# Expert layers of a two-block transformer kernel: 40 stored units for 64, one product for four key rows, 28 of 64 gate groups on ScalarE, three parked pairs

## The chip, the cores and the metric

The kernel runs on one core of a Trainium2 chip. Each engine (TensorE, VectorE, ScalarE, GpSimd, and SyncE, which issues the DMAs here) works through a queue of its own in order and waits on semaphores. The metric is the device time of one execution in microseconds (us). In the trace PE is TensorE's matmuls, PEld its weight loads, DVE VectorE, ACT ScalarE, POOL GpSimd and SP SyncE.

## The reference

Two transformer blocks run over 256 tokens of width 1024 in fp32. The change touches the feed-forward part of the first block's two layers, a product-key expert layer with 128 x 128 experts. Cut to that:

```python
def peer_ffn(x, norm_ffn, w_query, sub_keys, expert_down, expert_up):
    xn = rmsnorm(x, norm_ffn)
    def chunk(xi):                      # 128 tokens
        q = (xi @ w_query).reshape(B, 128, 8, 2, 128)
        s = jnp.einsum('bthpd,hpnd->bthpn', q, sub_keys)
        s1, i1 = lax.top_k(s[..., 0, :], 16)
        s2, i2 = lax.top_k(s[..., 1, :], 16)
        cand = s1[..., :, None] + s2[..., None, :]
        top_s, top_c = lax.top_k(cand, 16)       # over the 256 sums
        idx = i1[top_c // 16] * 128 + i2[top_c % 16]
        g = softmax(top_s)
        u = expert_down[idx]
        act = gelu(einsum('btd,bthkd->bthk', xi, u))
        return einsum('bthk,bthkd->btd', g * act, expert_up[idx])
```

`first_block` is mixer, expert layer, mixer, expert layer; `second_block` has gated feed-forward layers and further mixers, and its modulation vectors come from products with `w_mod`.

## The kernel before, in words

The kernel does not gather experts. `peer` computes all 16384 of them for all tokens and weights them with a dense gate matrix that is zero where an expert was not chosen. Experts are cut into 128 **units** of 128; unit `i` holds the experts whose second key index is `i`. A unit of `down` or `up` weights is 128x1024 fp32 (512 KB). `Stream.unit` loads it into one of three `raw` buffers, rounds it to `whi` on ScalarE (L93) and puts the remainder into `wlo` on VectorE (L97). `mm3` (L170 to L172) multiplies by three products, high by high, high by low and low by high, so a unit is 24 matmuls of 256 columns on TensorE, for `down` (tile `dn`) and for `up` (tiles `acc`) alike.

One expert layer runs in four parts.

1. **Routing.** Sixteen query units, scores, and on VectorE a long run of top-16 searches that ends with `it`: for each token, in 128 rows (8 heads by 16 picks), the first index, the second index and the gate.
2. **Stored units.** The first `N_STORE` down units are computed in pairs, beside the routing and behind it. ScalarE's gelu writes each pair into `ca`. They need no routing result.
3. **Gate stage.** 64 groups of four tokens. For a group, `oa` (VectorE, L631) holds one-hot rows of the first index, `ob` one-hot rows of the second index times the gate. `ob` is made by VectorE (L636) or, in the groups marked `by_act`, by two ScalarE operations a token (L633, L634). TensorE multiplies `oa` by `ob` into a PSUM bank `gps` (L639), four matmuls that the trace shows as eight records. Then VectorE multiplies the stored columns of `ca` by the first `N_STORE` columns of `gps` (L641), in place, so the first such product waits for the last stored unit; ScalarE copies the other columns to `gg` (L642). `oa` and `ob` have three buffers each, `gps` four banks.
4. **Loop.** The other down units, in pairs: gelu in place in PSUM, multiplied into `gg` (L667). The up units follow at a lag of 16 and are added up in `acc`.

The accumulators of `acc` take the four banks of tag `ac`. Until the loop starts, these serve the stored pairs, then `N_PARK` **parked** pairs (the first pairs of the loop, computed during the gate stage and held in PSUM until `gg` is complete) and one bank for `mod`. `Mod.step` (L935, L940) is one product of a 512 KB piece of `w_mod` through the same three `raw` buffers, four matmuls shown as eight records. Eight steps make a row, which ends with a copy `mrow` (L944) and two transposes (L946). The first expert layer has 32 such steps behind its parked pairs, the second 40.

The order of each engine's queue is not written out: a planner of the framework sets it when the kernel is built, from priorities and a timeline of its own. A loop in the code therefore appears in the queues interleaved with its neighbours.

Of the kernel before, what the change touches and what calls it, by code (L numbers as in the profile page):

```python
# [14 lines left out]
OP = mybir.AluOpType  # L15
# [4 lines left out]
NDC = 8  # L20
EPS = 1e-6
NEG = -1.0e30
N_STORE = 64
N_LAG = 16
N_PARK = 2
N_MOD = 32
M_0 = 40
M_1 = 72
PAT_1 = "gggv"
PAT_0 = "gv"  # L30
M_BUFS = 3
N_ACT = 3
OH = 3
AB = 3
AHEAD = 0
# [452 lines left out]
def peer(n: Net, layer, mod, mod_upto):  # L488
    nc, d = n.nc, n.d
    pre = f"l{layer}_"  # L490
    NS = N_STORE
    n.stream.pattern = PAT_R
    with ExitStack() as st:
        sp = st.enter_context(n.tc.tile_pool(name="pk", bufs=1, reuse_waits="tile"))
        it = sp.tile([128, 3, T], F32, name="it")
# [4 lines left out]
        def down_pair(i, sink, tag=None):  # L500
            b = n.bank("dn", tag).rearrange("p (u t) -> p u t", u=2)
            for u in range(2):
                w = n.unit(d[pre + "down"][i + u])
                n.proj_t(b[:, u], w, xn, first=u == 0)
            sink(b)

        with ExitStack() as sr:
# [44 lines left out]
            for a0, a1, wb, o in CAND:  # L552
                na = a1 - a0
                nc.vector.tensor_tensor(
                    out=cand[:, :, o:o + na * wb].rearrange("p h (a b) -> p h a b", b=wb),
                    in0=v4[:, :, 0, a0:a1].unsqueeze(3).to_broadcast([128, 16, na, wb]),
                    in1=v4[:, :, 1, 0:wb].unsqueeze(2).to_broadcast([128, 16, na, wb]), op=OP.add)
            for h in range(16):
# [6 lines left out]
                                    op=OP.subtract)  # L565
# [15 lines left out]
            for a0, a1, wb, o in CAND[:-1]:  # L581
                run = r.tile([128, 16, 16], F32, tag="run", name="run", bufs=2)
                for i, s0 in enumerate(starts[a0 + 1:a1 + 1]):
                    if i == 0:
                        nc.vector.tensor_scalar(out=run, in0=pos, scalar1=float(s0), scalar2=None, op0=OP.is_ge)
                    else:
                        nc.vector.scalar_tensor_tensor(out=run, in0=pos, scalar=float(s0), in1=run,
                                                       op0=OP.is_ge, op1=OP.add)
# [5 lines left out]
            for s, rank in ((0, ra), (1, rb)):  # L594
                for k0, k1 in ((0, 4), (4, 8), (8, 16)):
# [3 lines left out]
                                            in1=n.iota[:, 0:k1].unsqueeze(1).unsqueeze(1).to_broadcast([128, 16, nk, k1]),  # L599
                                            op=OP.is_equal)  # L600
                    nc.vector.tensor_tensor(out=o, in0=o,
                                            in1=i4[:, :, s, 0:k1].unsqueeze(2).to_broadcast([128, 16, nk, k1]),
                                            op=OP.mult)
# [9 lines left out]
            for i in range(0, NS, 2):  # L613
                down_pair(i, lambda b: nc.scalar.activation(
                    out=ca[:, i:i + 2], in_=b, func=AF.Gelu_apprx_tanh), "ac")

        with ExitStack() as sg:
            gp = sg.enter_context(n.tc.tile_pool(name="gg", bufs=1, reuse_waits="tile"))
            gg = gp.tile([128, 128 - NS, T], F32, name="gg")
            onehot = n.tc.tile_pool(name="oneh", bufs=OH, reuse_waits="tile")  # L620
            o2 = onehot.__enter__()
            for t0 in range(0, T, 4):
                a = o2.tile([128, 4, 128], F32, tag="oa", name="oa")
                b = o2.tile([128, 4, 128], F32, tag="ob", name="ob")
                g = n.bank("gps").rearrange("p (t e) -> p t e", t=4)


                by_act = t0 // 4 % N_ACT == 1
                for t in range(4):
                    at = lambda s: it[:, s, t0 + t:t0 + t + 1]  # L630
                    nc.vector.tensor_scalar(out=a[:, t], in0=n.iota, scalar1=at(0), scalar2=None, op0=OP.is_equal)  # L631
                    if by_act:
                        nc.scalar.activation(out=b[:, t], in_=n.iota, func=AF.Abs, scale=-1.0, bias=at(1))  # L633
                        nc.scalar.activation(out=b[:, t], in_=b[:, t], func=AF.Relu, scale=-2.0, bias=at(2))  # L634
                    else:
                        nc.vector.tensor_scalar(out=b[:, t], in0=n.iota, scalar1=at(1), scalar2=at(2),  # L636
                                                op0=OP.is_equal, op1=OP.mult)
                for t in range(4):
                    nc.tensor.matmul(g[:, t], a[:, t], b[:, t], start=t == 0, stop=True, skip_group_check=True)  # L639
                ge = g.rearrange("p t e -> p e t")  # L640
                nc.vector.tensor_tensor(out=ca[:, :, t0:t0 + 4], in0=ca[:, :, t0:t0 + 4], in1=ge[:, 0:NS], op=OP.mult)  # L641
                nc.scalar.copy(out=gg[:, :, t0:t0 + 4], in_=ge[:, NS:128])  # L642
            n.stream.pattern = PAT_G
            onehot.__exit__(None, None, None)
            g2 = sg.enter_context(n.tc.tile_pool(name="gg2", bufs=2, reuse_waits="tile"))

            def coef(i):
                return ca[:, i] if i < NS else gg[:, i - NS]

            acc = []  # L650

            def up(i):
                if not acc:
                    acc.extend(n.accs())
                w = n.unit(d[pre + "up"][i])
                c = coef(i)
                ch = g2.tile([128, T], F32R, tag="ch", name="ch")
                cl = g2.tile([128, T], F32R, tag="cl", name="cl")
                n.split(c, ch, cl)
                n.up(acc, w, (ch, cl), i == 0, i == 127)  # L660

            done = 0
            for i in range(NS, 128, 2):
                def sink(b):
                    nc.scalar.activation(out=b, in_=b, func=AF.Gelu_apprx_tanh)
                    c = gg[:, i - NS:i - NS + 2]
                    nc.vector.tensor_tensor(out=c, in0=c, in1=b, op=OP.mult)  # L667
                if i == NS + 2 * N_PARK:
                    while mod.next < mod_upto:
                        mod.step(n.main.raw_p)  # L670
                    mod.bank = None
                down_pair(i, sink, "ac" if i < NS + 2 * N_PARK else None)
                while i >= NS + 2 * N_PARK and done < i + 2 - N_LAG:
                    up(done)
                    done += 1
            while done < 128:
                up(done)
                done += 1
            n.residual(n.x, acc)
# [765 lines left out]
def two_blocks_kernel(ctx: ExitStack, tc: tile.TileContext, d, out, stages=None):  # L1445
# [12 lines left out]
    for s in stages:  # L1458
        with tc.tile_pool(name="xn", bufs=1, reuse_waits="tile") as n.xn_p:
            if s in ("mix0", "mix1"):  # L1460
                with n.psum(ac=4, mm=3, fl=1), tc.tile_pool(name="mod", bufs=M_BUFS, reuse_waits="tile") as p:
                    with n.low():
                        aside(mods[0], p, M_0 if s == "mix0" else M_1)
                    (hgrn_gmlp if s == "mix0" else mla_moba)(n)
            elif s.startswith("peer"):
                with n.psum(ac=4, mm=2, m2=2):
                    peer(n, int(s[4]), mods[1], N_MOD if s[4] == "0" else 72)
            elif s.startswith("mod"):
                with n.psum(ac=4, mm=2, fl=2), tc.tile_pool(name="mod", bufs=3, reuse_waits="tile") as p:
                    aside(mods[int(s[3])], p, 72)  # L1470
            elif s.startswith("ffn"):
                w, l = int(s[3]), int(s[5])
                with n.psum(ac=4, mm=2, m2=2):
                    ffn(n, n.x, mods[l], 0, 0 if w == 1 else 6, d[f"f{w}i{l}"], d[f"f{w}o{l}"],
                        n.v(f"norm_g{l}")[:, (w - 1) * 16:(w - 1) * 16 + 8], s)
            elif s == "mixb0":
                with n.psum(ac=4, mm=2, fl=2):
                    window_gla(n, mods[0])
            elif s == "mixb1":
                with n.psum(ac=4, mm=2, m2=2):  # L1480
                    pool_mix(n, mods[1])
            elif s == "final":
                with n.psum(ac=4, mm=2, m2=2):
                    final_norm(n, out)
# [154 lines left out]
```

## Time and profile before

| | us |
|---|---|
| median of three runs | 3464.38 |
| lowest of three | 3463.34 |
| the profiled execution | 3467.64 |
| its span in the trace | 3465.9 |

The profiled execution is 3.3 us above the median, and its span is 1.7 us below its own time. One of the three times, 13268.22 us, is far off and plays no part here. Times below are us from the start of the span. Matmuls are pipelined, so a record's length is more than the time until the next one starts, and a busy share close to 1 can hide slack; idle time and the distances between starts say more.

### The profile page before, as it was taken

The numbers are of one execution on the slowest core, as the hardware profiler recorded it, in microseconds if no ns is written. First come the engines' busy times: TensorE is split into PE (matmuls) and PEld (weight loads), VectorE is DVE, ScalarE is ACT, GpSimd is POOL, SyncE is SP. The second block draws the span as 40 slices with busy tenths as digits, with TensorE's granted clock in tenths as the row PEclk, the third lists the DMA queues.
The fourth block names the chain that finished last, engine by engine and source line by source line (L and its number), as shares of the span: only waits on it lengthen the run. The fifth ranks groups of instructions, "written<-read, shape, count | busy, mean of one in ns | idle before, by whom it ended". The sixth has DMA issues, their size and how long they took to land.

```text
span 3465.9 us, 65621 instructions
## 1 busy us (share of the span) xinstructions
PE 3313.4 (96%) x26734; PEld 3150.2 (91%) x26734; DVE 2193.9 (63%) x4589; ACT 1649.2 (48%) x2609; POOL 179.0 (5%) x93
## 2 busy tenths in 40 slices
PE   7999998999999999998999999999999989999798
PEld 6789977999999779996899999999999779999698
DVE  6389487555556559759555555666766656666665
ACT  5445455444444344445445444544644444454443
POOL 2200000000000310000000000100000020100200
PEclk9999999999999999999999999999999999999899
DMA  6645544556555545545556555554444235454353
GB/s 227 230 159 182 178 156 161 183 183 207 183 183 170 199 157 166 177 158 182 195 183 231 183 183 183 182 183 143 158 165 147 86 123 187 165 183 156 132 187 105
DMA packets 165759, 597.79 MB, mean 172 GB/s; under 512 B 18512, under 2 KB 20176, under 8 KB 165072
## 3 DMA queue, kind: packets, MB, share of 16 engines
q1 hardware_dynamic: 165456, 593.59, 51.5%
q8 instruction: 210, 3.44, 0.4%
q14 instruction: 93, 0.76, 0.1%
HBM read 592.47 MB, written 1.05 MB: 171 GB/s over the span
## 4 chain that ended last, share of the span: by engine, by line
PE 83%; DVE 11%; DMA 2%; ACT 2%; issue 1%; POOL 0%; SPq 0%; ACTq 0%; DVEq 0%; POOLq 0%
PE acc L170 11%; PE acc L171 10%; PE acc L172 10%; PE dn L172 7%; PE dn L170 7%; PE dn L171 7%; PE ff L170 6%; PE ff L171 6%; PE ff L172 6%; DVE wlo L97 2%; PE mm L170 2%; PE mm L171 2%; PE mm L172 2%; PE mod L940 2%; DMA mraw<-w_mod 2%; PE gps L639 2%
## 5 line engine op out<-in xcount | busy, mean ns | idle before, releaser
L93 ACT CAST whi<-raw 128x1024 fp32r<-128x1024 f32 x973 | 1016.3, 1046 | 1398.9 <-PE acc L171 540.7
L97 DVE TENSOR_TENSOR wlo<-raw,whi 128x1024 fp32r<-128x1024 f32 x908 | 1111.6, 1225 | 841.8 <-ACT whi L93 841.3
L170 PE MATMUL dn<-xnh,whi 128*128 128x256 f32 x2048 | 582.3, 284 | 3.1 <-ACT gg L642 2.5
L172 PE MATMUL dn<-xnh,wlo 128*128 128x256 f32 x2048 | 581.8, 285 | 1.5 <-DVE wlo L97 1.5
L171 PE MATMUL dn<-xnl,whi 128*128 128x256 f32 x2048 | 581.5, 284 | 0.0
L171 PE MATMUL acc<-cl,whi 128*128 128x256 f32 x2048 | 561.6, 283 | 1.0 <-DVE cl L165 1.0
L172 PE MATMUL acc<-ch,wlo 128*128 128x256 f32 x2048 | 559.5, 283 | 0.0
L170 PE MATMUL acc<-ch,whi 128*128 128x256 f32 x2048 | 512.2, 283 | 0.2 <-DVE gg L667 0.2
L170 PE MATMUL ff<-xnh,whi 128*128 128x258 f32 x1760 | 504.6, 287 | 7.5 <-ACT rstd L216 4.0
L171 PE MATMUL ff<-xnl,whi 128*128 128x258 f32 x1760 | 502.8, 286 | 4.2 <-DVE xnl L247 4.2
L172 PE MATMUL ff<-xnh,wlo 128*128 128x258 f32 x1760 | 499.2, 284 | 3.5 <-POOL wlo L97 2.2
L170 PEld LDWEIGHTS dn<-xnh,whi 128*128 128x128 f32 x2048 | 395.0, 193 | 3.7 <-ACT gg L642 2.7
L172 PEld LDWEIGHTS dn<-xnh,wlo 128*128 128x128 f32 x2048 | 394.4, 193 | 2.2 <-DVE wlo L97 2.2
L171 PEld LDWEIGHTS dn<-xnl,whi 128*128 128x128 f32 x2048 | 395.0, 193 | 0.0
L171 PEld LDWEIGHTS acc<-cl,whi 128*128 128x128 f32 x2048 | 393.2, 192 | 1.5 <-DVE cl L165 1.5
L172 PEld LDWEIGHTS acc<-ch,wlo 128*128 128x128 f32 x2048 | 392.1, 192 | 0.0
L170 PEld LDWEIGHTS acc<-ch,whi 128*128 128x128 f32 x2048 | 363.7, 192 | 0.4 <-DVE gg L667 0.4
L170 PEld LDWEIGHTS ff<-xnh,whi 128*128 128x128 f32 x1760 | 334.8, 190 | 12.2 <-ACT rstd L216 5.2
L171 PEld LDWEIGHTS ff<-xnl,whi 128*128 128x128 f32 x1760 | 337.0, 192 | 6.3 <-DVE xnl L247 5.6
L172 PEld LDWEIGHTS ff<-xnh,wlo 128*128 128x128 f32 x1760 | 335.1, 191 | 4.9 <-POOL wlo L97 2.7
L97 POOL TENSOR_TENSOR wlo<-raw,whi 128x1024 fp32r<-128x1024 f32 (+1 forms) x65 | 157.7, 2433 | 2614.0 <-ACT whi L93 1968.6
L171 PE MATMUL acc<-hl,whi 128*128 128x256 f32 x880 | 246.9, 282 | 3.0 <-DVE hl L1017 3.0
(446 smaller groups left out, 5389.5 us busy)
## 6 DMA issues: line engine op xcount, KB each, us to landing
raw<-l_down SPq DMA_DIRECT2D x256, 512.0 KB, 3.4
raw<-l_up SPq DMA_DIRECT2D x256, 512.0 KB, 3.3
mraw<-w_mod SPq DMA_DIRECT2D x144, 512.0 KB, 4.4
raw<-f1i SPq DMA_DIRECT2D x132, 512.0 KB, 3.4
raw<-f2i SPq DMA_DIRECT2D x88, 512.0 KB, 3.9
raw<-f1o SPq DMA_DIRECT2D x66, 512.0 KB, 3.3
raw<-w_t SPq DMA_DIRECT2D x46, 512.0 KB, 3.6
raw<-f2o SPq DMA_DIRECT2D x44, 512.0 KB, 4.1
```

Source lines behind the costliest of these rows:

```text
L93: nc.scalar.copy(hi[:, 0:k], raw[:, 0:k])
L97: eng.tensor_tensor(out=low[:, 0:k], in0=raw[:, 0:k], in1=hi.bitcast(F32)[:, 0:k], op=OP.subtract)
L170: mm(out, w[0], x[0], start=first, stop=False, skip_group_check=True)
L171: mm(out, w[0], x[1], start=False, stop=False, skip_group_check=True)
L172: mm(out, w[1], x[0], start=False, stop=last, skip_group_check=True)
L639: nc.tensor.matmul(g[:, t], a[:, t], b[:, t], start=t == 0, stop=True, skip_group_check=True)
L940: nc.tensor.matmul(ps[32 * j:32 * j + 32], n.cond[:, k], raw[:, j * T:(j + 1) * T], start=k == 0, stop=k == NDC - 1, tile_position=(0, 32 ...
```

## The change

`N_STORE` goes from 64 to 40, so 24 down units of each expert layer move from before the gate stage into the loop; `ca` shrinks to 40 columns and `gg` grows from 64 to 88. `oa` is made by one product of 512 elements for a group where there were four of 128. `N_ACT` becomes 7 and the test for `by_act` changes, so ScalarE makes `ob` in 28 of the 64 groups where it made 21; they lie 3, 2, 2, 3, 2, 2, 2 groups apart. `N_PARK` goes from 2 to 3.

```diff
-N_STORE = 64
+N_STORE = 40
 N_LAG = 16
-N_PARK = 2
+N_PARK = 3
...
-N_ACT = 3
+N_ACT = 7
...
                 g = n.bank("gps").rearrange("p (t e) -> p t e", t=4)
...
-                by_act = t0 // 4 % N_ACT == 1
+                by_act = t0 // 4 * N_ACT % 16 < N_ACT
+                nc.vector.tensor_tensor(out=a, in0=n.iota.unsqueeze(1).to_broadcast([128, 4, 128]),
+                                        in1=it[:, 0, t0:t0 + 4].unsqueeze(2).to_broadcast([128, 4, 128]),
+                                        op=OP.is_equal)
                 for t in range(4):
                     at = lambda s: it[:, s, t0 + t:t0 + t + 1]
-                    nc.vector.tensor_scalar(out=a[:, t], in0=n.iota, scalar1=at(0), scalar2=None, op0=OP.is_equal)
                     if by_act:
```

In the changed kernel the lines behind this place are numbered two higher, and `oa` is made in L629.

VectorE's queue in the middle of the first layer's gate stage, before:

```order
L641 TENSOR_TENSOR ca<-ca,gps 128x64x4
L631 TENSOR_SCALAR oa<-iota,it 128x128 x4
L641 TENSOR_TENSOR ca<-ca,gps 128x64x4
L631 TENSOR_SCALAR oa<-iota,it 128x128
L636 TENSOR_SCALAR ob<-iota,it 128x128
L631 TENSOR_SCALAR oa<-iota,it 128x128
```

and after:

```order
L643 TENSOR_TENSOR ca<-ca,gps 128x40x4
L629 TENSOR_TENSOR oa<-iota,it 128x512
L638 TENSOR_SCALAR ob<-iota,it 128x128 x4
L643 TENSOR_TENSOR ca<-ca,gps 128x40x4
L629 TENSOR_TENSOR oa<-iota,it 128x512
L643 TENSOR_TENSOR ca<-ca,gps 128x40x4
```

A group whose `ob` VectorE makes was nine instructions and is six; a group of ScalarE's was five and is two.

ScalarE's queue at about the same place, before:

```order
L633 ACTIVATE ob<-iota,it 128x128 x4
L634 ACTIVATE ob<-ob,it 128x128 x2
L642 COPY gg<-gps 128x64x4
L634 ACTIVATE ob<-ob,it 128x128 x2
L642 COPY gg<-gps 128x64x4 x2
```

and after:

```order
L635 ACTIVATE ob<-iota,it 128x128 x4
L644 COPY gg<-gps 128x88x4
L636 ACTIVATE ob<-ob,it 128x128 x4
L635 ACTIVATE ob<-iota,it 128x128 x4
L644 COPY gg<-gps 128x88x4
L636 ACTIVATE ob<-ob,it 128x128
L644 COPY gg<-gps 128x88x4
L636 ACTIVATE ob<-ob,it 128x128 x3
L644 COPY gg<-gps 128x88x4 x2
```

Before, three copies stand between the start of one gated group and that of the next; now mostly two.

TensorE's queue at the end of the second layer's gate stage, where `dn` is the first pair of the loop, before:

```order
L639 MATMUL gps<-ob,oa 128x128 x2
L940 MATMUL mod<-mraw,cond 32x256 x4
L639 MATMUL gps<-ob,oa 128x128
L940 MATMUL mod<-mraw,cond 32x256 x4
L946 MATMUL mod<-ident,mrow 128x128 x2
L170 MATMUL dn<-xnh,whi 128x256
```

and after:

```order
L641 MATMUL gps<-ob,oa 128x128 x10
L948 MATMUL mod<-ident,mrow 128x128 x2
L641 MATMUL gps<-ob,oa 128x128 x6
L942 MATMUL mod<-mraw,cond 32x256 x32
L948 MATMUL mod<-ident,mrow 128x128 x2
L170 MATMUL dn<-xnh,whi 128x256
```

The last row of `w_mod`, eight steps in one piece, now stands behind the last gate group, where one step stood. In the first layer the last step stays ahead of the last groups. Further up, the twelve `gps` matmuls of the fifth to seventh gate group stand in a row in all four queues (in the trace they are 24 records in a row); ahead of this place the queue of the first layer has 590 `dn` matmuls fewer than before, that of the second 594, and the loop 528 more each. Between this place and the first step of `w_mod` stand 40 `dn` matmuls before, up to the tenth group, and 102 and 106 after, up to the eighteenth.

## Rows read from the trace of the kernel before

**Rows 1.** The page, part 1: busy time of each engine and its instructions.
```profile
PE 3313.4 (96%) x26734; PEld 3150.2 (91%) x26734; DVE 2193.9 (63%) x4589; ACT 1649.2 (48%) x2609; POOL 179.0 (5%) x93
```
**Rows 2.** Stretches: window, length, busy PE, PEld, DVE, ACT, POOL, clock, DMA share, GB/s.
```profile
360.00:440.00 80.00, 80.00 (x669) 80.00 (x669) 33.67 (x29) 36.32 (x42) 0.00 (x0) 1.00 0.54 182
449.50:572.00 122.50, 106.89 (x813) 78.95 (x812) 109.81 (x457) 67.93 (x216) 0.00 (x0) 0.94 0.47 155
1537.50:1658.00 120.50, 107.22 (x849) 75.43 (x847) 106.60 (x455) 65.31 (x213) 0.00 (x0) 0.96 0.51 167
```
**Rows 3.** The chain that ended last, both expert layers: start, length, piece.
```profile
449.53 2.68 PE gps L639 x24
...
575.21 0.38 PE acc L170
...
581.07 0.48 PE acc L170 x4
583.95 0.48 PE acc L170 x4
...
1537.50 2.68 PE gps L639 x24
...
1670.05 0.12 PE acc L170
```
**Rows 4.** Timeline of VectorE in the first gate stage: start, length, instruction.
```profile
519.64 0.86 DVE L631 TENSOR_SCALAR oa<-iota,it 128x128 f32<-128x128 f32 x4
520.42 0.41 DVE L641 TENSOR_TENSOR ca<-ca,gps 128x256 f32<-128x256 f32 x1
520.75 0.27 DVE L631 TENSOR_SCALAR oa<-iota,it 128x128 f32<-128x128 f32 x1
520.95 0.33 DVE L636 TENSOR_SCALAR ob<-iota,it 128x128 f32<-128x128 f32 x1
521.21 0.27 DVE L631 TENSOR_SCALAR oa<-iota,it 128x128 f32<-128x128 f32 x1
```
**Rows 5.** VectorE's groups by shape, 300 to 345 us: count, busy us, mean ns.
```profile
L598 DVE TENSOR_TENSOR oh<-rb,iota 128x2048 f32<-128x2048 f32 x1 | 2.3, 2294 | 0.0
...
L598 DVE TENSOR_TENSOR oh<-ra,iota 128x512 f32<-128x512 f32 x1 | 0.7, 693 | 0.0
```
**Rows 6.** Timeline of ScalarE in the first gate stage.
```profile
524.12 1.28 ACT L633 ACTIVATE ob<-iota,it 128x128 f32<-128x128 f32 x4 [2.88 <-PE gps L639]
525.30 1.26 ACT L634 ACTIVATE ob<-ob,it 128x128 f32<-128x128 f32 x4
526.47 0.62 ACT L642 COPY gg<-gps 128x256 f32<-128x256 f32 x2
```
**Rows 7.** Waits between 445 and 578 us: total us, times, longest.
```profile
ACT ob L633 <- PE gps L639: 25.7, 12, 3.7
...
DVE ca L641 <- PE gps L639: 12.6, 9, 3.0
...
PE mod L940 <- DMA mraw<-w_mod: 7.4, 8, 1.8
```
**Rows 8.** The w_mod row copies of the first stage, and TensorE's timeline of one row.
```profile
L944 DVE COPY mrow<-mod x4: 409/413/419, 477.0 to 548.6; 128x256 f32<-128x256 f32 x4
...
534.92 1.50 PE L940 MATMUL mod<-mraw,cond 128*32 128x256 f32 x24
...
539.30 0.64 PE L940 MATMUL mod<-mraw,cond 128*32 128x256 f32 x8 [0.99 <-DMA mraw<-w_mod]
...
544.96 0.42 PE L940 MATMUL mod<-mraw,cond 128*32 128x256 f32 x4 [1.28 <-DMA mraw<-w_mod]
```
**Rows 9.** End of the second gate stage: a stretch, and TensorE's timeline.
```profile
1660.00:1665.00 5.00, 3.93 (x16) 3.24 (x17) 3.35 (x7) 2.09 (x2) 0.00 (x0) 0.50 0.77 242
...
1657.27 0.64 PE L940 MATMUL mod<-mraw,cond 128*32 128x256 f32 x8
...
1661.21 0.58 PE L170 MATMUL dn<-xnh,whi 128*128 128x256 f32 x1 [0.60 <-ACT whi L93]
```

## The prediction, as made before the run

> **What bounds the kernel now.** I read the page's busy times first, then the stretches, the chain of waits, the timelines of the gate stage. TensorE is busy for 96% of the span [rows 1], so the change can win only where TensorE does no useful work. The stretches show two such places, the gate stages of the two expert layers. In the 80 us ahead of the first stage TensorE is busy throughout at a granted clock of 1.00, while VectorE works for 33.7 us only: routing is over, and the gates wait for stored units. From 449.5 to 572 us it is turned round: VectorE is busy for 109.8 of 122.5 us, ScalarE for 67.9, TensorE's weight loads for 79.0 [rows 2]. So the work that could cover the gate stage is spent before it.
>
> I measure a stage from the place where twelve `gps` matmuls start in a row (fifth gate group) to the first up matmul of `acc`. Before, that is 449.53 to 575.21, 125.7 us, and 1537.50 to 1670.05, 132.6 us [rows 3]. The kernel does the same matmuls after the change, so its gain is what these two stretches lose, corrected for units moved across their ends.
>
> **Moved units.** Twenty-four matmuls take 2.88 us (583.95 less 581.07) [rows 3], 0.12 us each. The 590 `dn` matmuls that leave the place ahead of the first stage free 70.8 us on the path, in full, since TensorE never idles there [rows 2]; the 528 that the loop gets cost 63.4 us. The loop must stay bound by TensorE for that: a pair there gets one gelu and one product more than a stored pair, while VectorE and ScalarE have half their time free beside a TensorE that is full, as in the 80 us above (33.7 and 36.3 busy). I cost these at nothing; without the cover each would be some 0.7 us a pair (a 512-element operation [rows 5]), 8 us a layer. The difference, 62 matmuls or 7.4 us (66 or 7.9 us in the second layer), is the further parked pair, now inside the stage.
>
> **VectorE's share of a group.** Starts lie 0.78 us apart over four pieces of `oa`, 0.26 over a piece of `ob`, 0.33 over `ca` [rows 4]. A group of VectorE's took 0.78 + 1.04 + 0.33 = 2.15 us, one of ScalarE's 1.11; with 43 and 21 of them, 1.81 on average. The one product of 512 elements is not in the trace, but a comparison of the same form is: 693 ns at 512 elements and 2294 at 2048, so 1.042 ns an element [rows 5]. `ca`'s 0.33 for 256 elements then leaves 0.06 for the instruction, and `oa` takes 0.60, `ca` with 160 elements 0.23. Groups now take 1.87 and 0.83, and 36 and 28 of them 1.42 on average: 0.39 less, 23.6 us for the 60 groups behind the mark. Bounds: with 0.69 for `oa` and nothing saved at `ca`, 12 us; 24 is the other end. I take 23.6, since spacing and not length is what repeats.
>
> Here a rule speaks against the edit. The rows give 0.78 for four pieces and 0.60 for the one. The Trainium skill, "VectorE: DVE Perf Modes", section "The perf-mode tier table (the rule you actually need)", says that an fp32 tensor_scalar in SBUF runs at two elements a cycle and an fp32 tensor_tensor at one; its cycle table in the section "The TRN2 errata — SBUF-src ops pay a fixed extra latency per instruction" gives as an estimate 4 x 0.13 = 0.51 us for the pieces and 0.59 for the one. By the page the edit would cost 0.09 a group, not save 0.18, and the forecast below would be 3462. The trace agrees on the one product (the page has 2293 ns at 2048 elements, the row 2294) but not on the pieces, and the row decides.
>
> **ScalarE's share.** Its `ob` for a group takes 2.35 us (524.12 to 526.47), and two `gg` copies 0.62 [rows 6]. Seven more groups add 16.5 us over 64. `gg` grows from 256 elements to 352: nothing if its time is fixed, 0.12 if all of it goes by the element; I take 0.08. Together 0.34 a group, 20 us a stage, so 67.9 becomes some 91 with the whi and gelu of 2.6 further parked units. VectorE's 109.8 becomes 109.8 - 23.6 + 2.9 (wlo of those units, 1024 elements at the slope above) = 89. TensorE has 60 groups at 0.89 (24 records in 2.68 [rows 3]), 53.6 us, 102 `dn` matmuls, 12.2, and 32 steps of `w_mod` at 0.5 (three in 1.50 [rows 8]), 16: 82. So three engines come out nearly level where one stood out.
>
> **What the stage takes then.** Before, VectorE idled 12.7 of 122.5 us; the waits of that stage are VectorE's for TensorE, 12.6 us, and behind them TensorE's for `w_mod`, 7.4 us [rows 7]. Neither goes away. With three level engines, queues in order and three buffers I expect 14 us beside ScalarE's 91: 105 us to the last `ca`. Ends: 8 and 22, so 99 to 113.
>
> First layer: behind the last group the loop's first pair takes 48 x 0.12 = 5.8 us, and 0.7 passes at `gg`, so 111.5 against 125.7. With the 7.4 that is **21.6 us** gained.
>
> Second layer: the last row of `w_mod` now stands behind the last group, uncovered. Three steps are loaded (1.5 us); five more come as the buffers allow, three steps in 5.66 us (539.30 to 544.96, a wait for DMA ahead of both [rows 8]), so 9.4; from the start of the last step to the first `dn` 3.9 passed before (1657.27 to 1661.21 [rows 9]), of which 0.5 is counted. That is 14.3. Before it the granted clock was 0.50 of full speed, 1.2 of 2.4 GHz, while the first pair ran (1660 to 1665), after a TensorE that waited, and the pair took 8.8 us to 1670.05 [rows 3, 9]; it will again. 105 + 14.3 + 8.8 = 128.1 against 132.6, with the 7.9 **12.4 us** gained.
>
> Sum: 34 us. The profiled execution's 3467.64 becomes 3433.6; it lies 3.3 above the median, so on the median 3464.38 - 34 = **3430 us**.
>
> **The rivals.**
>
> *The w_mod stream sets the stage.* The first stage's row copies lie 71.6 us apart from the first to the fourth, 23.9 a row [rows 8], and VectorE needed 12 x 1.81 = 21.7 of it; now its 11.75 groups a row need 16.6. If the stream through three buffers does not get faster than 23.9, four rows take 96 us, and with 25 us for the 14 groups and parked units ahead of them (14 x 0.89 + 12.2) the stage takes 120, 15 more in each layer: 3460. For it: waits for `w_mod` are already there. Against: at three steps in 5.66 us, eight need 15.1, under 16.6.
>
> *The engines overlap well.* If parked pairs fill the waits and only 4 us stand beside ScalarE's 91, the stage takes 95, and the time is 3410. For it: VectorE lost little before. Against: then one engine was the bound, now three are.
>
> *The hand-off through ScalarE becomes the bound: slower.* ScalarE may start a group's `ob` only when the `gps` of three groups earlier has freed the buffer, and before it waited 25.7 us in 12 waits for just that [rows 7]. Most gated groups now lie two apart. If each is done in series, `gps` 0.89, `ob` 2.35, two `gg` at 0.39, `ca` 0.23, two groups take 4.25 us instead of ScalarE's own 3.1, three groups VectorE's 4.55; sixteen groups take 30.4, 60 take 114, and with the 13 of the other waits the stage takes 127: 22 more in each layer, 3474, slower than before. It decides from 122 us a stage on, that is when two groups take about 4.0. Against: the queue starts `ob` a group or two ahead, and a third buffer is there to hide it.
>
> *The one product takes its whole recorded 0.69 us and `ca` saves nothing*, the lower bound above: VectorE is then busy for 101 us, ten more than ScalarE, and with the 14 the stage takes 115, 3450. The two rows on spacing speak against it.
>
> That the change does not do what it says can be left out: the queues show the units moved.
>
> **How the numbers follow.** Forecast 0.55 (3416 to 3447 from the 99 and 113), w_mod stream 0.14, good overlap 0.17, hand-off 0.12, dear product 0.02. For 8 in 10 I take 3402 to 3464: it holds the forecast, the w_mod case and most of the good overlap, and leaves out the hand-off. Two per cent, about what a measurement of this kernel tells from no change, is 69 us. A gain of that size would need both stages at 88 us, under the busy time of their busiest engines: 0.04. A loss of it would need 35 us more in each stage than before: 0.02. Within: 0.94.
>
> **What the profile after would show.** The twelve `gps` some 71 us earlier, near 379 us; `oa` at 0.60 from start to start; TensorE busier and ScalarE's busy share near 0.87 in the stage; from there to the first up matmul 111 us in the first layer and 128 in the second, with eight steps of `w_mod` alone at its end. The forecast is wrong if the time from mark to last `ca` is not near 105: at 120 with TensorE waiting for `mraw` it is the stream, at 127 with TensorE waiting for ScalarE's `ob` the hand-off. It would also be wrong if the loop, now with 40 pairs behind the parked and first ones instead of 29, did not keep TensorE full.

## The result, and the profile after

The changed kernel takes 3427.94 us in the median of five runs (3419.31 to 3431.81), the kernel before 3464.38; the ratio is 0.9889 with an interval of 0.9874 to 0.9904. That is 36 us, 34 were forecast, and it lies inside two per cent. The profiled execution took 3422.14 us, the one before 3467.64: this pair is 45.5 us apart, more than the medians, so the places below add up to 45.5 and not to 36.

TensorE keeps its 26734 matmul records. The page, part 1, against [rows 1]:

```profile
PE 3278.1 (96%) x26734; PEld 3132.8 (92%) x26734; DVE 2157.5 (63%) x4173; ACT 1685.3 (49%) x2721; POOL 177.6 (5%) x93
```

The stretches from the mark (twelve `gps` matmuls in a row) to the last `ca`, and one behind the second stage; columns as in [rows 2]:

```profile
379.20:479.20 100.00, 95.22 (x850) 76.32 (x849) 88.81 (x263) 85.11 (x264) 0.00 (x0) 1.00 0.54 183
1433.60:1534.90 101.30, 94.61 (x859) 76.42 (x857) 88.13 (x263) 84.36 (x264) 0.00 (x0) 1.00 0.53 179
...
1535.00:1555.00 20.00, 11.60 (x86) 5.86 (x82) 6.35 (x12) 4.11 (x6) 0.00 (x0) 0.66 0.78 255
```

The marks and the end of the second stage in the chain, against [rows 3, 9]:

```profile
379.24 2.68 PE gps L641 x24
...
484.83 0.48 PE acc L170 x4
...
1433.64 2.68 PE gps L641 x24
...
1534.51 0.61 PE mod L942 x8
1535.14 4.11 DMA mraw<-w_mod
1539.30 0.68 PE mod L942 x8
1540.00 4.37 DMA mraw<-w_mod
1544.41 1.12 PE mod L942 x8
1545.55 3.27 DMA raw<-l_down
1548.84 1.05 ACT whi L93
...
1558.16 0.12 PE acc L170
```

From mark to first up matmul these are 105.6 and 124.5 us, where 125.7 and 132.6 stood. The reader should see three busy engines in the first two stretches, where VectorE alone stood out before ([rows 2]). The chain of work that ended last says the same: in the first stage VectorE's `oa`, `ob` and `ca` made up 18.6, 16.3 and 8.9% of it before and 1.0% or less each after, when TensorE's `gps` has 31.9%, the loads of `w_mod` 23.0% and ScalarE's `ob` 12.2%. The reader should also see, in the second layer, the eight `w_mod` steps behind the last group, from 1534.51 on: there the chain passes from load to product to load, and the first pair's load of `l_down` comes last (1545.55).

VectorE and ScalarE inside the stage, against [rows 4, 6]:

```profile
426.79 0.68 DVE L629 TENSOR_TENSOR oa<-iota,it 128x512 f32<-128x512 f32 x1
427.39 1.11 DVE L638 TENSOR_SCALAR ob<-iota,it 128x128 f32<-128x128 f32 x4
428.42 0.31 DVE L643 TENSOR_TENSOR ca<-ca,gps 128x160 f32<-128x160 f32 x1
428.65 0.68 DVE L629 TENSOR_TENSOR oa<-iota,it 128x512 f32<-128x512 f32 x1
```

```profile
425.70 0.45 ACT L644 COPY gg<-gps 128x352 f32<-128x352 f32 x1
426.03 0.42 ACT L636 ACTIVATE ob<-ob,it 128x128 f32<-128x128 f32 x1
426.33 0.45 ACT L644 COPY gg<-gps 128x352 f32<-128x352 f32 x1
426.66 1.01 ACT L636 ACTIVATE ob<-ob,it 128x128 f32<-128x128 f32 x3
```

`oa` starts 0.60 us ahead of the next instruction and `ca` 0.23, as the prediction had them; a `gg` copy holds ScalarE for 0.33. The waits between 370 and 490 us, against [rows 7], and the row copies of the first stage, against [rows 8]:

```profile
ACT ob L635 <- PE gps L641: 11.3, 12, 2.2
DVE ca L643 <- PE gps L641: 11.0, 16, 2.0
```

```profile
L946 DVE COPY mrow<-mod x4: 416/416/417, 418.5 to 474.6; 128x256 f32<-128x256 f32 x4
```

VectorE waits about as long as before (12.6 us then), ScalarE less than half (25.7), and a row of `w_mod` takes 18.7 us where it took 23.9.

Outside the stages the trace gives a layer's length by where the last sum of `x` (L209) at its end starts. After:

```profile
L209 DVE TENSOR_TENSOR x<-acc,x x8: 410/412/425, 181.2 to 184.7; 128x256 f32<-128x256 f32 x8
L209 DVE TENSOR_TENSOR x<-acc,x x8: 406/411/424, 1082.8 to 1085.8; 128x256 f32<-128x256 f32 x8
L209 DVE TENSOR_TENSOR x<-acc,x x8: 410/410/419, 1242.1 to 1244.5; 128x256 f32<-128x256 f32 x8
L209 DVE TENSOR_TENSOR x<-acc,x x8: 407/409/412, 2157.6 to 2164.5; 128x256 f32<-128x256 f32 x8
```

So the first expert layer runs from 184.7 to 1085.8, 901.1 us, the second from 1244.5 to 2164.5, 920.0. In the same rows of the kernel before the last sums start at 185.9, 1117.1, 1275.3 and 2209.6: 931.2 and 934.3. The gain is 30.1 us in the first layer and 14.3 in the second; the rest, 1 us, is no part of either.

### The profile page after: what moved, and what is told of

The parts are those of the page before. It is cut to its first block, busy times and chain, and to the rows that moved or that the text cites. A ratio compares the mean times of both kernels' runs of the same rounds, so it can differ in the third digit from the quotient of the medians.

```text
span 3420.4 us, 65219 instructions
## 1 busy us (share of the span) xinstructions
PE 3278.1 (96%) x26734; PEld 3132.8 (92%) x26734; DVE 2157.5 (63%) x4173; ACT 1685.3 (49%) x2721; POOL 177.6 (5%) x93
## 4 chain that ended last, share of the span: by engine, by line
PE 84%; DVE 8%; DMA 3%; ACT 2%; issue 1%; ACTq 0%; DVEq 0%
PE acc L170 11%; PE acc L171 11%; PE acc L172 10%; PE dn L172 7%; PE dn L170 7%; PE dn L171 7%; PE ff L170 6%; PE ff L171 6%; PE ff L172 6%; DMA mraw<-w_mod 2%; PE gps L641 2%; DVE wlo L97 2%; PE mm L170 2%; PE mm L171 2%; PE mm L172 2%; PE mod L942 2%
## 5 line engine op out<-in xcount | busy, mean ns | idle before, releaser
L172 PE MATMUL acc<-ch,wlo 128*128 128x256 f32 x2048 | 566.4, 283 | 0.0
L170 PE MATMUL acc<-ch,whi 128*128 128x256 f32 x2048 | 533.8, 283 | 0.0
L170 PEld LDWEIGHTS acc<-ch,whi 128*128 128x128 f32 x2048 | 373.1, 192 | 0.0
```

The source lines that it names most:

```text
L170: mm(out, w[0], x[0], start=first, stop=False, skip_group_check=True)
L172: mm(out, w[1], x[0], start=False, stop=last, skip_group_check=True)
```

## The experiments

Theory A, the prediction's: VectorE, the busiest engine of the gate stage, sets its length, so an edit is worth what it takes off VectorE, until ScalarE and TensorE are level with it; moved units change little. Rivals: B, the stored units kept back as cover are the gain; C, the `w_mod` stream sets the stage; D, the kernel before merely lost time to stretches at half the granted clock.

All twelve runs, with both kernels. *Stage* is from the start of the first `ca` product to that of the last, both layers (it begins some 4 us ahead of the mark), *VectorE* its busy time in there, *layer* as above, from one trace each; the ratio is to the kernel before on the same chip.

| kernel | stage | VectorE | layer | median | ratio |
|---|---|---|---|---|---|
| before | 125.7, 123.9 | 113.1, 109.9 | 931.2, 934.3 | 3464.38 | 1 |
| before again | 122.4, 123.9 | 113.0, 109.9 | 927.9, 934.1 | 3467.24 (one run) | - |
| before, 40 stored | 113.5, 111.3 | 107.0, 103.7 | 914.4, 925.0 | 3447.72 | 0.9964 (0.9947 to 0.9981) |
| before, one product | 111.0, 108.1 | 103.6, 100.1 | 917.0, 917.5 | 3437.03 | 0.9935 (0.9917 to 0.9954) |
| before, 28 groups | 112.5, 113.5 | 107.2, 104.2 | 918.1, 924.5 | 3448.05 | 0.9950 (0.9929 to 0.9971) |
| before, 3 parked | 120.5, 117.7 | 115.6, 113.0 | 921.1, 931.7 | 3461.62 | 1.0000 (0.9986 to 1.0013) |
| changed | 103.8, 104.5 | 91.8, 91.3 | 901.1, 920.0 | 3427.94 | 0.9889 (0.9874 to 0.9904) |
| changed, 64 stored | 106.0, 106.0 | 96.6, 96.3 | 908.0, 924.7 | 3436.89 | 0.9926 (0.9910 to 0.9942) |
| changed, four pieces | 110.1, 110.8 | 99.3, 99.5 | 915.5, 931.1 | 3451.23 | 0.9969 (0.9955 to 0.9984) |
| changed, 21 groups | 107.6, 103.6 | 99.1, 96.8 | 905.4, 922.5 | 3434.22 | 0.9925 (0.9908 to 0.9943) |
| changed, 32 groups | 112.4, 113.1 | 91.8, 88.6 | 907.0, 918.4 | 3432.28 | 0.9918 (0.9902 to 0.9934) |
| changed, no `w_mod` in layer 1 | 97.2, 103.2 | 90.8, 90.6 | 891.8, 985.7 | 3485.55 (one run) | - |
| changed, row in the mixer | 104.6, 105.2 | 91.9, 91.9 | 900.3, 921.2 | 3431.64 | 0.9904 (0.9887 to 0.9921) |
| changed, row among stored units | 107.9, 105.5 | 92.0, 90.1 | 906.2, 933.0 | 3439.69 | 0.9938 (0.9924 to 0.9951) |

A layer in a single trace can be off by some 5 us: the last kernel has the changed kernel's TensorE order throughout the first layer, and that layer came out at 906.2 against 901.1, its stage at 107.9 against 103.8. Smaller differences are read from the medians.

The columns show something that A leaves out. VectorE's busy time goes down by what the edits take off it: 6.1, 9.5 and 5.9 us for the first three parts alone and 2.5 more for the parked pair, 19.0 together in the first stage, and 21.3 in the changed kernel (18.7 and 18.6 in the second). But each part alone shortens the stage by more than that, because VectorE's idle time in the stage falls as well: from 12.7 and 14.0 us (9.3 and 14.1 in the second execution) to between 4.7 and 9.3. In the changed kernel it is back at 12.0 and 13.1, so the whole gains what comes off VectorE and no idle time.

**The parts one by one.** The units alone:

```diff
-N_STORE = 64
+N_STORE = 40
```

> The kernel before with 40 stored units alone. An expert layer is measured in the trace from the last residual of its mixer to its own: 931.2 and 934.3 us before, 901.1 and 920.0 after the whole change. Theory A (VectorE sets the gate stage, so a part is worth what it takes off VectorE, and moving units across the stage frees as much at one end as it costs at the other): 0.10 us less for ca in 60 groups, 6 us a layer, so about 925 and 928, median 3452. Theory B (the units that were spent ahead of the stage are the gain, since gates start 70 us earlier): at least 25 us in the first layer, 906 or less, median 3430 or less. Theory C (the w_mod stream sets the stage): 0 to 2 us a layer.

3447.72, ratio 0.9964, 12 us. Its stages from mark to last `ca` are 109.9 and 107.6 us, VectorE busy for 103.95 of the first. By the ratio this is A's number, and B's median of 3430 or less is not reached. The first layer of the trace, 914.4 us, lies between the two (A 925, B 906): its stage fell by 12.2 us where VectorE's busy time fell by 6.1.

The one product alone:

```diff
+                nc.vector.tensor_tensor(out=a, in0=n.iota.unsqueeze(1).to_broadcast([128, 4, 128]),
+                                        in1=it[:, 0, t0:t0 + 4].unsqueeze(2).to_broadcast([128, 4, 128]),
+                                        op=OP.is_equal)
...
-                    nc.vector.tensor_scalar(out=a[:, t], in0=n.iota, scalar1=at(0), scalar2=None, op0=OP.is_equal)
```

> The kernel before with oa made by one product a group alone. Theory A: 0.18 us off VectorE in 60 groups, 11 us a layer, so about 920 and 923, median 3442. Theory B and theory C: under 3 us a layer, since waits for TensorE or for w_mod take the place of VectorE's work. If the rule held that the four pieces run at twice the rate for an element, it would be 5 us slower a layer: 936 and 939.

3437.03, ratio 0.9935, 22 us: the largest part, and by the ratio A's 11 us a layer; the layers of the trace, 917.0 and 917.5, came out some 3 and 5 us shorter than A had them. By the cycle table of the Trainium skill that the prediction weighed ("VectorE: DVE Perf Modes", section "The TRN2 errata — SBUF-src ops pay a fixed extra latency per instruction") the edit would have been slower, and it is not.

ScalarE's groups alone:

```diff
-N_ACT = 3
+N_ACT = 7
...
-                by_act = t0 // 4 % N_ACT == 1
+                by_act = t0 // 4 * N_ACT % 16 < N_ACT
```

> The kernel before with ScalarE making 28 gated groups of 64 instead of 21, alone. Theory A: seven groups at 1.04 us off VectorE, 7 us a layer, about 924 and 927, median 3450; ScalarE has room, 68 of 122 us busy plus 16. Theory C and the hand-off through ScalarE: under 2 us, or slower, with TensorE waiting longer for ScalarE's ob.

3448.05, ratio 0.9950, 17 us, where A gave 14.

The parked pair alone:

```diff
-N_PARK = 2
+N_PARK = 3
```

> The kernel before with three parked pairs alone. Theory A: 48 matmuls, 5.8 us, leave the loop for the stage, where TensorE has idle time, and VectorE gets two units' wlo, 2.3 us: about 3.5 us faster in the first layer (928). In the second, five or six steps of w_mod now stand behind the last group, some 8 us without cover: 934.3 - 3.5 + 8, about 939, so a median near 3465. Theory B (cover is what the stage lacks): 6 us or more in the first layer.

```profile
451.60:568.50 116.90, 104.87 (x858) 80.00 (x857) 112.28 (x459) 69.41 (x218) 0.00 (x0) 1.00 0.48 163
1529.80:1643.20 113.40, 101.54 (x856) 77.03 (x854) 109.02 (x457) 66.72 (x216) 0.00 (x0) 1.00 0.50 166
```

3461.62, ratio 1.0000. Alone it is worth nothing in the median, as A said. The trace goes another way: VectorE is busier than before (112.28 and 109.02 against 109.8 and 106.6 [rows 2]), and yet the stages from mark to last `ca` are 5.6 and 7.1 us shorter (116.90 and 113.40 against 122.5 and 120.5), with the granted clock at 1.00 where it was 0.94 and 0.96. The first layer is 10.1 us shorter than before and 6.8 shorter than in the second execution, where A had 3.5 and B, cover as what the stage lacks, 6 or more. So waits were worth several us in the old stage beside VectorE's work, and with one more parked pair as cover they shrank. The four add up to 52 us by their ratios; together, in the changed kernel, they give 38.

**The kernel before once more**, unchanged, for its stretches at a lower clock.

> The kernel before once more, unchanged. In its profiled execution the granted clock stood at half for 6.8 us inside the first gate stage and again at its end, and for 3.4 and 6.8 us in the second, and VectorE idled 12.7 and 13.9 us; with any one part of the change there was one such window at most and 4 to 8 us of idle time. Theory D (these windows and the idle time around them are an accident of one execution, and part of the first layer's 30 us is): the stages take 112 to 117 us from mark to last ca, the first expert layer 920 to 925. Theory A as it stands (they belong to the order of the kernel before): 120 to 123, and 929 to 933 for the layer, with half clock in the stage again.

```profile
452.28:571.10 118.82, 105.21 (x811) 77.41 (x810) 109.75 (x457) 67.74 (x216) 0.00 (x0) 0.97 0.49 160
1540.66:1661.00 120.34, 106.41 (x849) 74.88 (x847) 106.54 (x455) 65.15 (x212) 0.00 (x0) 0.96 0.52 167
```

The mean granted clock is again under 1.00 in both stages, at 0.97 and 0.96 ([rows 2] have 0.94 and 0.96; the changed kernel has 1.00). So these stretches come again with the old stage and are no accident that the change happened to miss. The first stage takes 118.8 us, between D's 117 and A's 120, and the first layer 927.9, just under A's 929: part of the first stage's idle time does differ from one execution to the next. What the stretches at half clock cost by themselves was not measured.

**The units taken back out of the whole.**

```diff
-N_STORE = 40
+N_STORE = 64
```

> The changed kernel with 64 stored units again, the other parts kept. Theory A: VectorE's ca 0.10 us longer in 60 groups, ScalarE's gg 0.08 shorter, so the stages go from 100 and 101 to 102 to 106 us and the layers are 2 to 6 us longer each, median 3432 to 3440. Theory B (starting the gates earlier is the gain): 15 us or more a layer, 3458 or more.

3436.89, ratio 0.9926 against 0.9889: the 24 units are worth 13 us in company as alone. VectorE's busy time from mark to last `ca` rises from 88.8 to 93.0. The stages account for 2.2 and 1.5 us of it only. B as the account of the whole gain is out: it needed 3458 or more.

**The one product taken back out.**

```diff
-                nc.vector.tensor_tensor(out=a, in0=n.iota.unsqueeze(1).to_broadcast([128, 4, 128]),
...
+                    nc.vector.tensor_scalar(out=a[:, t], in0=n.iota, scalar1=at(0), scalar2=None, op0=OP.is_equal)
```

> The changed kernel, with key rows made in four products of 128 elements again and the rest kept. A: VectorE takes 0.78 us for a group's four instead of 0.59, 0.19 x 60 groups = 11 us more, busy about 100 instead of 88.5; stages 105 to 111 instead of 100 and 101, each layer 5 to 10 us longer, median 3438 to 3448. The rule of the perf modes (four tensor_scalar in fp32 at 2x, 0.51 a group by its table, against one tensor_tensor at 1x): VectorE 5 us less busy, median 3416 to 3428. TensorE as the bound (95 us busy in the changed stage): nothing moves, 3426 to 3430.

VectorE's timeline of this kernel, and the chain at the end of its first stage:

```profile
431.10 0.87 DVE L631 TENSOR_SCALAR oa<-iota,it 128x128 f32<-128x128 f32 x4
431.89 0.16 DVE L950 TENSOR_TENSOR mod<-mod,vec 128x8 f32<-128x8 f32 x1
```

```profile
484.55 4.65 DMA mraw<-w_mod
489.24 0.68 PE mod L940 x8
489.94 3.45 DMA raw<-l_down
493.41 1.06 ACT whi L93
```

3451.23, ratio 0.9969: 28 us slower than with the one product, more than any theory gave. The direction is A's: four pieces hold VectorE for 0.79 us. The other two theories of the expectation, 3416 to 3428 and, with TensorE as the bound, 3426 to 3430, are out. The stage accounts for 6.3 us in each layer (110.1 and 110.8 against 103.8 and 104.5). Another 7 lie behind the last `ca`: the planner now leaves more of `w_mod` there, and the first pair's load of `l_down` comes after it, through the same three buffers (489.94). A did not have that: the same edit that gave VectorE more work also left TensorE's queue in another order.

**ScalarE's share, up and down.** Every second group, 32 of 64:

```diff
-N_ACT = 7
+N_ACT = 8
```

> The changed kernel, with ScalarE making the gated rows of every second group (32 of 64) instead of 28. A: VectorE loses another 4 x 0.33 us = 1.3 us a stage and more of its waits may go; stage 98 to 101, median 3422 to 3432. Hand-off through ScalarE sets the stage (85 us busy of 100, four further groups of about 1.5 us on it bring 91): stage 103 to 108, layers 3 to 7 us longer, median 3434 to 3442.

From mark to last `ca`:

```profile
380.70:487.70 107.00, 95.74 (x847) 75.38 (x846) 88.61 (x253) 94.97 (x292) 0.00 (x0) 1.00 0.56 188
1444.70:1552.40 107.70, 99.62 (x904) 76.30 (x906) 85.40 (x250) 92.44 (x290) 0.00 (x0) 1.00 0.59 197
```

The old rule, 21 of 64:

```diff
-N_ACT = 7
+N_ACT = 3
...
-                by_act = t0 // 4 * N_ACT % 16 < N_ACT
+                by_act = t0 // 4 % N_ACT == 1
```

> The changed kernel, with the old rule for ScalarE (every third group, 21 of 64). A: VectorE gets 7 groups of gated rows back, about 0.9 us each with its reads of the gate, 6 to 7 us more busy (95 instead of 88.5); stages 103 to 107, layers 3 to 7 us longer, median 3434 to 3442. Hand-off through ScalarE sets the stage: ScalarE falls to 70 busy, stage 95 to 99, median 3418 to 3426. TensorE as the bound: within 2 us of 3428.

With 32 groups the stage takes 107 us from the mark, within the 103 to 108 of the hand-off through ScalarE, and ScalarE is busier than VectorE. The first layer loses 6 us; the second loses none, since the longer stage takes in `w_mod` steps that else stand behind it. The median, 3432.28, lies between the two expectations, and its interval overlaps that of the changed kernel by a hair. With 21 groups the ratio is 0.9925, 12 us slower, and the median inside A's range. So beyond 28 groups ScalarE and no longer VectorE sets the stage. That VectorE does so up to 28 is shown for the first layer only: with 21 groups VectorE is 7.3 and 5.5 us busier, and the first stage is 3.8 us longer, the second 0.8 shorter.

**The w_mod stream taken out of the first layer.** All 72 steps then stand in the second.

```diff
-N_MOD = 32
+N_MOD = 0
```

> The changed kernel with no w_mod step in the first expert layer and all 72 in the second. First stage: theory A (three level engines, VectorE and ScalarE at 89 and 85 us busy) gives 93 to 97 us instead of 100, since only 16 us of TensorE's and the 2.7 us of waits for mraw go; theory C (the stream sets the stage) gives 90 or less. Second stage: 42 steps instead of eight stand behind the last group. If bare steps cost 1.9 us each, the layer goes from 920 to about 985 us; if 0.5 each, to 937.

The first stage without steps, and a stretch of the second layer's tail:

```profile
379.18:472.50 93.32, 80.17 (x606) 74.14 (x606) 87.80 (x251) 86.30 (x267) 0.00 (x0) 0.98 0.10 35
...
1530.00:1610.00 80.00, 44.84 (x333) 9.52 (x331) 6.42 (x23) 1.63 (x5) 0.00 (x0) 0.53 0.77 253
```

Without a single step the stage still takes 93.3 us, with VectorE busy for 87.8 of it: A's number, and C falls, which needed 90 or less. The 32 steps cost the stage 7 us, though TensorE spends 16 on them (32 at 0.5 [rows 8]) and their loads are 23% of its chain. Bare, they cost far more: the second layer grew by 65.7 us for 32 steps, 2.05 each.

**The tail of the second layer.** The eight steps behind the last group take 16.6 us up to the chain's first `dn` product (1534.6 to 1551.2), and TensorE is busy for 8.2 of it: the one loss in the changed kernel that the rows show plainly. Two kernels move that row elsewhere. First, ahead of the layer, at the end of the second mixer:

```diff
+                        if s == "mix1":
+                            aside(mods[1], p, N_MOD + 8)
+                            mods[1].tag = "ac"
```

> The changed kernel with the last row of w_mod (eight steps) moved out of the second expert layer into the mixer ahead of it, at low priority. Theory A (the row behind the last gate group is bare time): the second gate stage then ends like the first, 5.7 us from the last ca to the first up matmul where 23.3 passed, so that layer falls from 920 to about 903 us; the mixer, 158.7 us with TensorE's weight loads 72% busy, pays 0 to 4 us; median 3412 to 3416. Rival: the mixer's own w_mod stream sets its time, eight further steps cost 1.9 us each there, 15 us, and nothing is won.

```profile
1236.46 6.55 DMA mraw<-w_mod
1243.05 0.68 PE mod L942 x8
1243.75 8.55 DMA mraw<-w_mod
1252.34 1.12 PE mod L942 x8
```

The tail is gone (last `ca` at 1552.6, the loop's first pair right behind it), but the row runs bare at the mixer's end, as this chain shows, and the mark comes 207.9 us behind the mixer's last sum instead of 189.1. The layer takes 921.2 us, ratio 0.9904: not told apart from the changed kernel.

Second, one step in every second pair among the stored units:

```diff
             for i in range(0, NS, 2):
+                if layer == 1 and i >= 8 and i % 4 == 0:
+                    mod.tag = "m2"
+                    mod.step(n.main.raw_p)
                 down_pair(i, lambda b: nc.scalar.activation(
                     out=ca[:, i:i + 2], in_=b, func=AF.Gelu_apprx_tanh), "ac")
 
+        mod.bank, mod.tag = None, "ac"
```

> The changed kernel, with the first of the second layer's w_mod rows taken out of the gate stage: its eight steps stand one in every second pair among the stored units. A (VectorE sets the gate stage; what a layer costs is its stage, its loops and what is left behind its last group): the second layer loses the tail that it ends on (1534.6 to 1551.2 us in the changed kernel, 16.6 us against 5.9 between last group and first loop product in the first layer), pays 8 x 0.5 us of TensorE among the stored units, stage unchanged at 100 to 102; layer 904 to 910 us instead of 920, median 3412 to 3420, 0.996 to 0.998 of the changed kernel. C (the w_mod stream sets the stage): the stage itself also falls, by 10 us or more, to 90 or less, layer under 900, median under 3408. If the steps among the stored units wait for their row as they do at the mixer's end, the layer stays at 920 or over.

SP's queue, a wait of ScalarE for the stored units, and the stretch:

```profile
1330.35 0.33 SPq L941 DMA_DIRECT2D mraw<-w_mod  x1
1332.75 12.17 SPq L85 DMA_DIRECT2D raw<-l_down  x4
1346.62 0.33 SPq L941 DMA_DIRECT2D mraw<-w_mod  x1
```

```profile
ACT whi L93 <- DMA raw<-l_down: 28.4, 15, 6.3
```

```profile
1345.00:1395.00 50.00, 39.22 (x271) 35.09 (x270) 44.31 (x94) 17.11 (x22) 0.00 (x0) 0.86 0.44 148
```

3439.69, ratio 0.9938: slower than the changed kernel, and A's 3412 to 3420 is wrong. The tail went, as expected: the time behind the last `ca` fell by 17.7 us (629.9 to 612.2). But the time from the mixer's end to the mark rose from 189.1 to 219.9. A piece of `w_mod` is loaded at 1330.35, and the first two steps on TensorE run together at 1375.78, behind matmuls that wait for routing and units. The first piece keeps one of three `raw` buffers for 45 us, the second (1346.62) another for 29; meanwhile the units go on with one, and ScalarE waits 28.4 us for their loads, a wait that the changed kernel does not have in that part. That the kept buffers are the cause was read from these rows; a fourth buffer was not tried.

## Why the prediction was right, step by step

**The place and the mechanism** hold. The marks moved to where they were forecast (379.24 for 379), the loop stayed bound by TensorE (busy for 600.5 of 601.0 us in the first layer, 600.9 of 606.3 in the second), and the changed kernel's stages are shorter by 21.9 and 19.4 us for 21.3 and 18.6 less of VectorE's busy time. In the medians single edits too are worth about what they take off VectorE in both stages (12, 22 and 17 us for 12, 19 and 12 less; the parked pair gives 0 for 6 more); that their stages fell by more, with the idle time, is not in the prediction.

The nearness of 34 to the 36 of the medians is in part luck. The terms were read from one trace, and on the pair of traces the two layers gained 44.4 us, 10 more than forecast; the changed kernel's profiled execution lies 5.8 us below its median, the one before 3.3 above.

**Moved units.** Forecast 70.8 us less ahead of the first mark and 63.4 more in the loop, 7.4 net. Measured 69.1 (263.6 to 194.5 behind the mixer's end) and 59.1 (541.9 to 601.0), 10.0 net. In the second layer 73.1 and 66.8, 6.3 net, for a forecast of 7.9. These differences lie within the spread of single traces.

**VectorE's share** came out as summed: 89 forecast, 88.81 and 88.13 measured. The pieces against the one product were decided by the row, 0.78 for 0.60; one edit alone (22 us faster) and the same edit undone (28 us slower) bear the row out. It is not the rate of the pieces that the rule against the edit had wrong. A tensor_scalar that multiplies each partition by a number of its own stands in the trace of the kernel before at two sizes (count, busy us, mean ns, idle us):

```profile
L705 DVE TENSOR_SCALAR pr<-pr,sm 128x512 f32<-128x512 f32 x16 | 7.7, 482 | 0.4
L705 DVE TENSOR_SCALAR pr<-pr,sm 128x128 f32<-128x128 f32 x8 | 2.3, 285 | 0.2
```

That is 197 ns for 384 further elements, 0.51 ns an element, half of the 1.04 of the one product [rows 5]. The Trainium skill, "VectorE: DVE Perf Modes", section "The perf-mode tier table (the rule you actually need)", has the same two rates, so the trace agrees with it there. What fails is the fixed part, the same for both forms in the cycle table that the prediction used. At 0.51 ns an element a piece of `oa`, 0.195 us from start to start, has 0.13 us that do not go by the element, and a piece of `ob`, which reads two numbers per partition, 0.19; the one product has 0.06. Four pieces pay 0.52 us in fixed parts alone.

**ScalarE's share** was the term mis-sized: 91 forecast, 85.1 and 84.4 measured, so that VectorE stayed the busiest engine. The parts were right, 16.4 us more for `ob` (47.81 to 64.21 in records of that tile alone) and 4.1 for `gg` (20.40 to 24.50, 4.8 forecast). But I added them to a busy time that counts overlapping records once. Before, the four tiles' records add up to 72.3 us for 67.9 busy; after, to 94.5 for 85.1. The closer the instructions stand, the more their records overlap.

**The stage** is the step that came out short for it: 105 forecast, 100 and 101 measured. The 14 us of waits beside ScalarE were 14.9 and 16.9, and VectorE idles for 11.2 and 13.2 us where it idled for 12.7 and 13.9. So the first layer gained 30.1 instead of 21.6 us (5.9 from the stretch, 2.6 from the moved units), the second 14.3 instead of 12.4 (3.6 from the stretch, less 1.6).

**The second layer's tail** was forecast at 23.1 us from the last `ca` to the first up matmul, eight steps and a first pair at 1.2 GHz, and took 23.6 (1534.6 to 1558.16), with a mean granted clock of 0.66 from 1535 to 1555. Its parts were a little further off and cancel: 15.3 us to the first `dn` for 14.3, and 8.2 for the pair for 8.8, in which matmuls start 0.21 us apart up to 1553.9 and 0.12 from there on.

**The rivals.** The `w_mod` stream: refuted by 93.3 us without it, and by rows of 18.7 us where the rival needed 23.9. Good overlap, 95 us: five short of the truth. The hand-off through ScalarE: not at 28 groups, but four groups on it is there (107 us with 32), so it lay nearer than its price of 127 us said. The dear product: `oa` holds VectorE for 0.60 us, not for its recorded 0.68.

**What stays open.** The parts alone add up to 52 us, the whole gives 38. The stages show where the surplus lies: alone, the four take 45 us off each, 19 of VectorE's busy time and 26 of its idle time, while the whole takes 22 and 19 off. Why any single edit sheds idle time and all four together do not was not settled. Undoing units, product and ScalarE's share one at a time costs 13, 28 and 12 us, 53 together; the stages have only some 19 of these, 14 more are the longer `w_mod` tail of the build with four pieces, and the rest was not placed. The third parked pair in company of the others was not undone. No kernel here beats the changed one.

## What to carry to other kernels

Where one engine stands out in a stage, a change there is worth about what it takes off that engine, until the next ones are level; then moving work either way wins nothing (32 groups and 21 were both no faster than 28), and a further gain needs less work in the stage, not another share-out. Read each edit's busy time beside its time: the engine's idle time (5 to 14 us of a stage here) moves with any edit, so gains of single edits do not add up. Many small instructions pay their fixed part each time, whatever their rate by the element. Add instructions to an engine's records by tile, and not to a busy time in which records overlap. Work that fills gaps is not free elsewhere: before moving it, look at what it shares (a queue, a pool of buffers) with the work at its new place, and how long it will hold it.

## What the runs showed of the hardware

- Bare products fed by 512 KB loads through three buffers cost 2.05 us each (65.7 us for 32 more of them behind the last group), and TensorE's granted clock was 0.53 over 80 us of them (1530 to 1610): mostly 1.2 GHz, with eight records of a step then at 1.08 us where they take 0.64 at the other level. The eight steps behind the changed kernel's last group start 1.7 us apart in the mean (1534.44 to 1546.64).
- Between the same two instruction orders on TensorE, one layer differed by 5 us (901.1 and 906.2), with TensorE's waits for `mraw` at 2.7 us in the one and 7.0 in the other. The waits are 4.3 of the 5 us; why the loads landed later was not looked into.
- VectorE's products with a number per partition run at 0.51 ns an element where a product of two tensors takes 1.04, but carry 0.13 us each that do not go by the element (0.19 with two such numbers, `ob`) where the other carries 0.06. So one product of 512 elements (0.60 us) beats four of 128 (0.78).
